# A hybrid decoder trunk on one core: the memory's row scales from loaded rows, and indexer scores of two heads' late rows in one matmul

## The chip, the core and the metric

The kernel runs on one core of one Trainium2 chip. A core has TensorE (PE in the profile, its weight loads PEld), VectorE (DVE), ScalarE (ACT), GpSimd (POOL) and SyncE (SP), which here only sends DMAs. Instructions of one engine run in the order in which they stand in its queue; engines wait for each other by semaphores. [...]

The metric is the device time of one execution in microseconds (us). Before the change three runs took 2596.93, 2597.0 and 2600.05 us; the median is 2597.0.

## The reference, cut to what matters

The trunk has four layers over 256 rows of 2048 features; mixers are latent attention, sparse attention, sliding window, latent attention. Each layer also attends with four heads to a memory of 256 rows. Two parts matter here.

First, the memory is normalised once, by rows, and every layer projects keys and values from it:

```python
mem_n = _rmsnorm(mem, mem_norm)      # y = x * rsqrt(mean(x*x, axis=-1) + EPS) * g
...
mem_out = _memory_attention(mq, mem_n @ w_mem_kv[i])
```

Second, the sparse mixer chooses 64 of 256 keys for each query row with an indexer of 16 heads of 64 numbers:

```python
k_top = min(IDX_TOPK_MAX, S // 4)    # 64
dots = jnp.einsum('bqhd,bkd->bqhk', iqb, ik, ...) * IDX_DIM ** -0.5
score = jnp.einsum('bqhk,bqh->bqk', jax.nn.relu(dots), iwb) * IDX_HEADS ** -0.5
score = jnp.where(qi[:, None] >= key_idx[None, :], score, NEG_INF)
_, sel = lax.top_k(score, k_top)
```

A query row below 64 has at most 64 keys that it may see, so all of them are chosen whatever the scores are. In the first tile of 128 query rows only the last 64 rows ("late rows") need scores.

## The kernel before

All matrices are float32. Each operand of a product is split into a high part, rounded to the type that TensorE reads at full rate, and a low part that holds the rest. A product is high x high + high x low + low x high. `parts_of` (L233) does this for weights: ScalarE copies 128x512 numbers to `wh` (L60), VectorE subtracts to get `wl` (L69), three buffers of each.

Weights stream from memory through five buffers `wr` of 512 KB (`stage`, L205); SP sends the loads. Two loops use them. `rows_by` (L239) gives rows of the result: features are stationary, a weight tile of 512 columns moves, three matmuls for each of 16 steps and two row tiles (L264 to L266). `columns_by` (L269) gives the result transposed: weights are stationary, both feature parts move together in 512 columns (L284), and the weights' low part takes 256 columns (L288). Each of the two holds two of the four accumulators (`acc`) in PSUM until its result is evicted.

The order of instructions on each engine comes from a planner, which runs through the program's order as priorities and issues what its own model of the times says is ready. `tc.keep_in_program_order` pins an instruction behind what was traced before it on its engine. Work that shall lie beside a matmul loop is written as a generator in the list `steps`; each loop calls `other_work` once per weight tile, which takes two steps (L228).

`memory()` (L363) comes first. The memory is given transposed as `l_mem`; four feature chunks `mft` (128x4x256, tag `pq`, five buffers) are loaded between the weights of the first `rows_by`, the values (`mv`) of layer 0's first half (`each`, L371; the last thing it sends is the constant `ident`), and are weighted and split in `prepare`. The row scale isn't needed for the product itself: it is applied when the accumulators are evicted, for values in `values` (L413) by rows with `mrstd`, for keys (`mk`) in `keys` (L423) by columns with `mbc`, which `spread` (L170) makes with two small products on TensorE. `row_scales` (L390) computes it from the feature chunks: four squares on ScalarE, pinned (L386), summed over chunks on VectorE (L388, L395, L396), summed over partitions on TensorE (`msr`, L400), then `rsqrt_mean` (L151), a chain of small VectorE instructions. It runs as steps in the first key block's `columns_by`; `values` of the first pass is one of its steps.

In layer 1, `select` (L802) computes the indexer's queries (`iqT`), keys (`ikd`) and head weights (`iw`). Twelve heads' queries of the first row tile are computed for its late rows alone (`stacked_late`); `iqT` holds zeros for the early rows of these heads, written by GpSimd (L809). High and low part of a head's 64 numbers lie on the two halves of the partitions, and `ikd` has the keys' high part twice and the low part twice in its two slices. `selection` (L856) is a generator of steps: for each row tile b and head, two matmuls of 256 columns (L865), Relu on ScalarE (L868), a scaled add on VectorE (L873). Then, eight times, the eight largest scores are found and taken out (L881, L882), and what remains becomes the mask `sel` (L885). At its end `spaced_values` makes the values' operand in the same buffers that `iqT` had. Its steps run in the loops of the memory queries, of the gate and of the first group's queries.

Of the kernel before, what the change touches and what calls it, by code (L numbers as in the profile page):

```python
# [31 lines left out]
def kernel(ctx: ExitStack, tc: tile.TileContext, a: dict, out: bass.AP,  # L32
# [39 lines left out]
    x = [cst.tile([P, D], F32, name=f"x{t}") for t in range(2)]  # L72
    xin = a["x"].rearrange("b (t p) d -> t p (b d)", p=P)


# [287 lines left out]
    def memory():  # L363
# [3 lines left out]
        mT = [act.tile([P, 2, 4, S], F32R, name="mT", tag=f"big{c}") for c in range(4)]  # L367
        sq = act.tile([P, 4, S], F32, name="msq", tag="aux", bufs=AUX)
        acc0 = []

# [11 lines left out]

        def squares(c):

            s1 = sq if c == 0 else act.tile([P, 4, S], F32, name="ms1", tag="aux", bufs=AUX)
            tc.keep_in_program_order(nc.scalar.activation(s1, mft[c].q, AF.Square))  # L386
            if c:
                nc.vector.tensor_add(sq, sq, s1)  # L388

        def row_scales():  # L390

            for c in range(4):
                squares(c)
                yield True
            nc.vector.tensor_add(sq[:, :2, :], sq[:, :2, :], sq[:, 2:, :])  # L395
            nc.vector.tensor_add(sq[:, 0, :], sq[:, 0, :], sq[:, 1, :])  # L396
            yield True
            pr = misc("msr")
            for t in range(2):
                nc.tensor.matmul(pr[:, t:t + 1], sq[:, 0, t * P:(t + 1) * P], ones[:, :1],  # L400
                                 start=True, stop=True)
            yield True
            s2 = small("ms2", 2)
            nc.vector.tensor_copy(s2, pr[:, :2])
            rsqrt_mean(mrstd, s2, D)
            nc.vector.tensor_scalar(m16, mrstd, 0.0625, None, op0=OP.mult)
            yield True
            values(0, 0, acc0[0])
            for _ in range(4):
                yield True  # L410
            spread(mbc, m16)
# [20 lines left out]
        for i in range(depth):  # L432
            w = a["w_mem_kv"][i]
            for p_ in range(2):
                begins = i == p_ == 0
                if begins:
                    pinned.append(0)
                    acc0.append(rows_by(mT, 16, w, 0, (MEMW, 512), "mv", prepare, each))
                    pinned.pop()
                    steps.append(row_scales())  # L440
                else:
                    values(i, p_, rows_by(mT, 16, w, 0, (MEMW + p_ * 512, 512), "mv"))
                for h in (2 * p_, 2 * p_ + 1):
                    acck = columns_by(mT, 16, w, 0, (h * 256, 256), "mk")
                    while begins and steps:
                        other_work()
                    keys(i, h, acck)
                step = 2 * i + p_
                if begins:

                    not_before(f32(mT[3])[:, 0, 3, :1])
                    late_constants()
                    bias_table(0)
                    bias_table(1)
                if 1 <= step < 5:
                    steps.append(nm.first_chunk(step - 1))


    def transposed(dst, srcs):

        for i0 in range(0, len(srcs), 4):
            i1 = min(len(srcs), i0 + 4)
            tp = misc("tr", F32R)
            for i in range(i0, i1):
                nc.tensor.transpose(tp[:, (i - i0) * P:(i - i0 + 1) * P], srcs[i], identr)
            copy_act(dst(i0, i1), f32(tp)[:, :(i1 - i0) * P].rearrange("p (j c) -> p j c", c=P))

# [275 lines left out]
    class Grouped:  # L743
# [46 lines left out]

        def stacked(self, dst, src, sc, n):

            s3 = src.rearrange("p (g d) -> p g d", g=n)
            for g0 in range(0, n, 4):
# [4 lines left out]
                transposed(lambda i0, i1: dst(g0 + i0, g0 + i1),  # L799
                           [hl[:, g].rearrange("p a b -> p (a b)") for g in range(4)])  # L800

        def select(self):  # L802
            nm, w = self.nm, self.w
            iqT = [act.tile([P, 8, S], F32R, name="iqT", tag=f"big{1 + z}") for z in range(2)]
            ikd = act.tile([P, 2, S], F32R, name="ikd", tag="kr", bufs=1)
            iw = small("iw", 32, bufs=2)

            for z, n in ((0, 8), (1, 4)):
                nc.gpsimd.memset(f32(iqT[z])[:, :n, :64], 0.0)  # L809
            late_x = act.tile([P, 16, 2, 64], F32R, name="xl64", tag="big3")  # L810
# [4 lines left out]
            for n in (8, 4, 4):  # L815
# [3 lines left out]
                for t in range(2):  # L819
                    sc = nm.col("rstd", t)  # L820
                    if late is not None and t == 0:
                        self.stacked_late(lambda i0, i1: iqT[h0 // 8][:, h0 % 8 + i0:h0 % 8 + i1, 64:P],
                                          acc[0][:, :n * 64], sc, n)
                        continue
                    sl = slice(t * P, (t + 1) * P)
                    self.stacked(lambda i0, i1: iqT[h0 // 8][:, h0 % 8 + i0:h0 % 8 + i1, sl],
                                 acc[t][:, :n * 64], sc, n)
                    if h0 == 12:
# [3 lines left out]
            nc.vector.tensor_scalar(iw, iw, 0.25, None, op0=OP.mult)  # L832
            return self.selection(iqT, ikd, iw)

# [20 lines left out]

        def selection(self, iqT, ikd, iw):  # L856

            for b in range(2):
                n = (b + 1) * P
                sco = [wk.tile([P, S], F32, name=f"sco{z}", tag=f"sco{z}", bufs=1) for z in range(2)]  # L860
                cur = 0
                for h in range(16):
                    sp = misc("isp")
                    for v in range(2):
                        nc.tensor.matmul(sp[:, :S], iqT[h // 8][:, h % 8, b * P:(b + 1) * P], ikd[:, v, :],  # L865
                                         start=v == 0, stop=v == 1)
                    rl = wk.tile([P, S], F32, name="rl", tag="e", bufs=4)
                    nc.scalar.activation(rl[:, :n], sp[:, :n], AF.Relu, scale=0.125)  # L868
                    c = iw[:, b * 16 + h:b * 16 + h + 1]
                    if h == 0:  # L870
# [5 lines left out]
                    yield True  # L876
                nc.vector.tensor_add(sco[1 - cur][:, :n], sco[cur][:, :n], caus[:, S - n:])
                cur = 1 - cur
                for it in range(8):
                    m8 = small("m8", 8)  # L880
                    nc.vector.max(m8, sco[cur][:, :n])  # L881
                    nc.vector.match_replace(sco[1 - cur][:, :n], m8, sco[cur][:, :n], TAKEN)  # L882
                    cur = 1 - cur
                    yield True
                nc.vector.tensor_scalar(self.sel[:, b, :n], sco[cur][:, :n], -2e38, NEG,  # L885
                                        op0=OP.is_gt, op1=OP.mult)
# [156 lines left out]
def _laid_out(inputs):  # L1043
# [6 lines left out]
    for name, o in (("mem_norm", 0), ("a_q_norm", 32), ("a_kv_norm", 56), ("norm_in", 64)):  # L1050
# [4 lines left out]

_INS = ["x", "final_norm", "rel_bias", "w_in_a", "w_uq",
        "w_ukv", "w_in_b", "w_in_c", "c_sinks", "w_mem_kv", "w_out"]
# [23 lines left out]
```

## Time and profile before

| | |
|---|---|
| runs | 2596.93, 2597.0, 2600.05 us |
| the profiled execution | 2597.13 us, of which the span 2595.3 |
| TensorE busy, share of the span | 2576.4 us, 99% |
| weight loads | 2216.7 us, 85% |
| VectorE | 1880.5 us, 72% |
| ScalarE | 1619.6 us, 62% |
| GpSimd | 68.0 us, 3% |
| mean granted TensorE clock | 0.998 |
| moved by DMA | 509.53 MB |

The busy time of TensorE is that of overlapping instructions: a matmul's own length is longer than the time by which it moves the next one. What a matmul costs is read from the chain that ended last, where each piece has only the time that it adds. A line number is that of the instruction in the code; where a helper records it (L60, L69, L202), the tile's name tells which use it is.

### The profile page before, as it was taken

Reading aid. Unit: us, or ns where it says so; the run is one execution under the profiler, and the core shown is the slowest. Engines: PE = TensorE matmul, PEld = TensorE weight load, DVE = VectorE, ACT = ScalarE, POOL = GpSimd, SP = SyncE. Lnnn points to the kernel's source line nnn. Section 1 sums busy time; section 2 is a strip of 40 time slices with the busy share of each in tenths; the row PEclk is TensorE's granted clock in tenths of the full one; section 3 lists DMA queues with packets and bytes.
Section 4 is the critical chain, followed back from the end, with each engine's and each line's share of the span. In section 5 each row is a group of like instructions: output and inputs, shape, how many; then the busy total and the mean of one; then the engine's idle time right before and its main releaser. Section 6 shows DMA issues by size and latency. Waiting matters only on the chain.

```text
span 2595.3 us, 41702 instructions
## 1 busy us (share of the span) xinstructions
PE 2576.4 (99%) x14066; PEld 2216.7 (85%) x14066; DVE 1880.5 (72%) x4130; ACT 1619.6 (62%) x3420; POOL 68.0 (3%) x124
## 2 busy tenths in 40 slices
PE   9999999999999999999999999999999999999997
PEld 7888898888888888888888888888888888888886
DVE  7666667667776686787778776777778767676667
ACT  6556556556656566667666666676666655665655
POOL 0100000000000010000000000000000000000000
PEclk9999999999999999999999999999999999999999
DMA  7888777666676667566556575555655766566664
GB/s 257 254 258 267 242 214 234 185 171 190 193 203 201 197 218 246 163 196 189 192 164 199 170 224 170 175 174 180 195 161 149 233 183 168 170 167 182 212 178 131
DMA packets 455128, 509.53 MB, mean 196 GB/s; under 512 B 68816, under 2 KB 351712, under 8 KB 453760
## 3 DMA queue, kind: packets, MB, share of 16 engines
q1 hardware_dynamic: 441392, 449.58, 57.9%
q0 software_dynamic: 13088, 56.16, 6.8%
q8 instruction: 110, 1.80, 0.3%
q10 hardware_dynamic: 432, 1.11, 0.1%
q14 instruction: 106, 0.87, 0.1%
HBM read 487.81 MB, written 31.56 MB: 200 GB/s over the span
## 4 chain that ended last, share of the span: by engine, by line
PE 99%; DVE 1%; ACT 0%; DMA 0%; SPq 0%; issue 0%; ACTq 0%
PE acc_g L284 14%; PE acc_g L288 7%; PE acc_wo L264 7%; PE acc_wo L265 7%; PE acc_wo L266 7%; PE acc_mk L284 5%; PE acc_mq L284 5%; PE acc_cq L284 3%; PE acc_qn L284 3%; PE acc_mq L288 2%; PE acc_mk L288 2%; PE acc_q L265 2%; PE acc_q L266 2%; PE acc_q L264 2%; PE acc_mv L265 2%; PE acc_mv L264 2%
## 5 line engine op out<-in xcount | busy, mean ns | idle before, releaser
L69 DVE TENSOR_TENSOR wl<-wr,wh 128x512 fp32r<-128x512 f32 (+2 forms) x1728 | 1165.0, 677 | 625.8 <-ACT wh L60 602.8
L60 ACT ACTIVATE wh<-wr 128x512 fp32r<-128x512 f32 (+2 forms) x1728 | 1070.4, 621 | 813.8 <-PE acc_g L284 179.3
L284 PE MATMUL acc_g<-xT,wh 128*128 128x512 f32 x1536 | 486.3, 396 | 0.0
L288 PEld LDWEIGHTS acc_g<-xT,wl 128*128 128x128 f32 x1536 | 284.8, 188 | 60.8
L288 PE MATMUL acc_g<-xT,wl 128*128 128x256 f32 x1536 | 310.5, 280 | 0.0
L265 PE MATMUL acc_wo<-wl,y 128*128 128x512 f32 x768 | 303.5, 395 | 0.2 <-DVE wl L69 0.2
L266 PE MATMUL acc_wo<-wh,y 128*128 128x512 f32 x768 | 298.2, 390 | 0.0
L284 PEld LDWEIGHTS acc_g<-xT,wh 128*128 128x128 f32 x1536 | 238.3, 189 | 4.4
L264 PE MATMUL acc_wo<-wh,y 128*128 128x512 f32 x768 | 240.1, 391 | 0.1
L265 PEld LDWEIGHTS acc_wo<-wl,y 128*128 128x128 f32 x768 | 144.3, 188 | 28.4 <-DVE wl L69 0.6
L266 PEld LDWEIGHTS acc_wo<-wh,y 128*128 128x128 f32 x768 | 144.3, 188 | 27.9
L264 PEld LDWEIGHTS acc_wo<-wh,y 128*128 128x128 f32 x768 | 142.2, 188 | 29.2 <-ACT y L60 1.0
L284 PE MATMUL acc_mk<-mT,wh 128*128 128x512 f32 x512 | 161.7, 396 | 0.3 <-DVE mv L418 0.3
L284 PE MATMUL acc_mq<-xT,wh 128*128 128x512 f32 x512 | 161.6, 396 | 0.0
L968 DVE TENSOR_TENSOR x<-x,acc_wo 128x512 f32<-128x512 f32 x192 | 126.1, 681 | 5.7 <-PE acc_wo L266 5.6
L284 PE MATMUL acc_qn<-cT,wh 128*128 128x512 f32 x384 | 121.2, 397 | 0.0
L284 PE MATMUL acc_cq<-xT,wh 128*128 128x512 f32 x384 | 120.8, 396 | 0.0
L288 PEld LDWEIGHTS acc_mk<-mT,wl 128*128 128x128 f32 x512 | 96.0, 188 | 22.3 <-DVE wl L69 0.4
L288 PEld LDWEIGHTS acc_mq<-xT,wl 128*128 128x128 f32 x512 | 94.0, 188 | 20.1
L288 PE MATMUL acc_mq<-xT,wl 128*128 128x256 f32 x512 | 103.3, 282 | 0.0
L288 PE MATMUL acc_mk<-mT,wl 128*128 128x256 f32 x512 | 101.9, 278 | 0.0
L265 PE MATMUL acc_q<-wl,xT 128*128 128x512 f32 x256 | 101.1, 395 | 0.0
(304 smaller groups left out, 4272.5 us busy)
## 6 DMA issues: line engine op xcount, KB each, us to landing
wr<-in_w_out_dram SPq DMA_DIRECT2D x192, 512.0 KB, 3.6
wr<-in_w_in_a_dram SPq DMA_DIRECT2D x176, 512.0 KB, 4.0
wr<-in_w_mem_kv_dram SPq DMA_DIRECT2D x120, 512.0 KB, 4.4
wr<-in_w_in_b_dram SPq DMA_DIRECT2D x112, 512.0 KB, 3.5
wr<-in_w_in_c_dram SPq DMA_DIRECT2D x104, 512.0 KB, 3.5
wr<-in_w_uq_dram SPq DMA_DIRECT2D x192, 128.0 KB, 2.5
wr<-in_w_uq_dram SPq DMA_DIRECT2D x48, 256.0 KB, 3.7
tab<-flat POOLq DMA_DIRECT2D x8, 1536.0 KB, 9.4
```

The costliest lines, as they stand in the source:

```text
L60: inst = nc.scalar.activation(o, i, AF.Copy, scale=scale)
L69: nc.vector.tensor_sub(lo, src, f32(hi))
L264: nc.tensor.matmul(acc[t][:, :n], xh, wh[:, :n], start=first, stop=False)
L265: nc.tensor.matmul(acc[t][:, :n], xh, wl[:, :n], start=False, stop=False)
L266: nc.tensor.matmul(acc[t][:, :n], xl, wh[:, :n], start=False, stop=last)
L284: nc.tensor.matmul(acc[j], wh[:, o:o + P], q[:, :, kt % 4, :], start=kt == 0, stop=False)
L288: nc.tensor.matmul(acc[j][:, 0, :], wl[:, o:o + P], q[:, 0, kt % 4, :], start=False, stop=kt == kts - 1)
L968: nc.vector.tensor_add(xs, xs, acc[t])
```

## The change

The memory's row scales. The memory is now an input in its own layout too (`mem`). Right after the first pass over the values has been traced, eight loads of 128x512 numbers (256 KB each) are pinned behind `ident` on SP's queue, into four tiles of the tag `pq`, which the feature chunks hold until they are split. After the whole first key block, in program order, `row_scales` squares each block on ScalarE with a sum along the row (`square_sum`, L202 of the kernel before), adds the four sums of each row on VectorE, and goes on as before to `rsqrt_mean` and `spread`; then `values` of the first pass are evicted, then the keys. The squares of the feature chunks, their sums on VectorE and the sum over partitions on TensorE are gone, and so are the steps.

Selection. `iqT` is now one tile for each row tile: for b = 0 16 heads x 64 late rows, for b = 1 16 heads x 128 rows. The last four heads of the first tile, which come for all rows, are transposed as before, and only the late half is copied out. For b = 0 the stationary operand holds the late rows of heads 2h and 2h + 1; the moving operand holds 128 keys' high parts and 128 keys' low parts, so one matmul of 256 columns gives both, side by side, where there were two matmuls for each head. ScalarE copies the one half, VectorE adds the other, then come Relu and the scaled add as before, for eight pairs instead of 16 heads. In the end the sum over even heads, on the first 64 partitions, is copied to the last 64 and added. Max, replace and mask work on the late rows alone; GpSimd clears the early rows of `sel`, and the clearing of `iqT` is gone.

```diff
+    min_ = a["mem"].rearrange("b (t p) d -> t p (b d)", p=P)
...
+        mss = small("mss", 8, bufs=2)
...
-        def squares(c):
-
-            s1 = sq if c == 0 else act.tile([P, 4, S], F32, name="ms1", tag="aux", bufs=AUX)
-            tc.keep_in_program_order(nc.scalar.activation(s1, mft[c].q, AF.Square))
-            if c:
-                nc.vector.tensor_add(sq, sq, s1)
-
-        def row_scales():
-
+        def memory_rows(c):
+            q = act.tile([P, 2, 512], F32, name="mrow", tag="pq", bufs=PQ)
+            for t in range(2):
+                tc.keep_in_program_order(
+                    nc.sync.dma_start(q[:, t, :], min_[t][:, c * 512:(c + 1) * 512]))
+            return q
+
+        def row_scales(mrow):
             for c in range(4):
-                squares(c)
-                yield True
-            nc.vector.tensor_add(sq[:, :2, :], sq[:, :2, :], sq[:, 2:, :])
-            nc.vector.tensor_add(sq[:, 0, :], sq[:, 0, :], sq[:, 1, :])
-            yield True
-            pr = misc("msr")
-            for t in range(2):
-                nc.tensor.matmul(pr[:, t:t + 1], sq[:, 0, t * P:(t + 1) * P], ones[:, :1],
-                                 start=True, stop=True)
-            yield True
+                for t in range(2):
+                    square_sum(mss[:, t * 4 + c:t * 4 + c + 1], mrow[c][:, t, :])
             s2 = small("ms2", 2)
-            nc.vector.tensor_copy(s2, pr[:, :2])
+            nc.vector.tensor_reduce(s2, mss.rearrange("p (t c) -> p t c", t=2), AX.X, OP.add)
             rsqrt_mean(mrstd, s2, D)
             nc.vector.tensor_scalar(m16, mrstd, 0.0625, None, op0=OP.mult)
-            yield True
-            values(0, 0, acc0[0])
-            for _ in range(4):
-                yield True
             spread(mbc, m16)
...
                     pinned.append(0)
-                    acc0.append(rows_by(mT, 16, w, 0, (MEMW, 512), "mv", prepare, each))
+                    acc = rows_by(mT, 16, w, 0, (MEMW, 512), "mv", prepare, each)
                     pinned.pop()
-                    steps.append(row_scales())
+                    mrow = [memory_rows(c) for c in range(4)]
...
                     acck = columns_by(mT, 16, w, 0, (h * 256, 256), "mk")
-                    while begins and steps:
-                        other_work()
+                    if begins and h == 0:
+                        row_scales(mrow)
+                        values(i, p_, acc)
                     keys(i, h, acck)
...
-            iqT = [act.tile([P, 8, S], F32R, name="iqT", tag=f"big{1 + z}") for z in range(2)]
+            iqT = [act.tile([P, 16, (64, P)[b]], F32R, name=f"iqT{b}", tag=f"big{2 - b}") for b in range(2)]
...
-            for z, n in ((0, 8), (1, 4)):
-                nc.gpsimd.memset(f32(iqT[z])[:, :n, :64], 0.0)
...
+            iw2 = small("iw2", 8, bufs=2)
+            pairs = iw[64:, :16].rearrange("p (h e) -> p h e", e=2)
+            for e in range(2):
+                nc.scalar.activation(iw2[64 * e:64 * e + 64], pairs[:, :, e], AF.Copy)
+            return self.selection(iqT, ikd, iw, iw2)
...
+            nc.gpsimd.memset(self.sel[:64, 0, :P], 0.0)
             for b in range(2):
                 n = (b + 1) * P
+                rows = slice(0, P) if b else slice(64, P)
...
-                for h in range(16):
+                for h in range((8, 16)[b]):
                     sp = misc("isp")
-                    for v in range(2):
-                        nc.tensor.matmul(sp[:, :S], iqT[h // 8][:, h % 8, b * P:(b + 1) * P], ikd[:, v, :],
-                                         start=v == 0, stop=v == 1)
                     rl = wk.tile([P, S], F32, name="rl", tag="e", bufs=4)
-                    nc.scalar.activation(rl[:, :n], sp[:, :n], AF.Relu, scale=0.125)
-                    c = iw[:, b * 16 + h:b * 16 + h + 1]
+                    if b == 0:
+
+                        nc.tensor.matmul(sp[:, :S], iqT[0][:, 2 * h:2 * h + 2, :].rearrange("p h c -> p (h c)"),
+                                         ikd[:, :, :P], start=True, stop=True)
+                        lo = wk.tile([P, S], F32, name="isl", tag="z", bufs=3)
+                        copy_act(lo[:, :P], sp[:, P:S])
+                        nc.vector.tensor_add(lo[:, :P], lo[:, :P], sp[:, :P])
+                        nc.scalar.activation(rl[:, :n], lo[:, :P], AF.Relu, scale=0.125)
+                        c = iw2[:, h:h + 1]
+                    else:
+                        for v in range(2):
+                            nc.tensor.matmul(sp[:, :S], iqT[1][:, h, :], ikd[:, v, :],
+                                             start=v == 0, stop=v == 1)
+                        nc.scalar.activation(rl[:, :n], sp[:, :n], AF.Relu, scale=0.125)
+                        c = iw[:, 16 + h:17 + h]
...
+                if b == 0:
+                    even = wk.tile([P, S], F32, name="isl", tag="z", bufs=3)
+                    nc.scalar.activation(even[64:, :n], sco[cur][:64, :n], AF.Copy)
+                    nc.vector.tensor_add(sco[cur][64:, :n], sco[cur][64:, :n], even[64:, :n])
```

29 lines of the change are left out of this document (13 added, 16 removed).

## The prediction

> **What bounds the kernel now.** I read the page's busy times first, then the chain that ended last, then stages of the span.
>
> ```profile
> span 2595.3 us, 41702 instructions
> PE 2576.4 (99%) x14066; PEld 2216.7 (85%) x14066; DVE 1880.5 (72%) x4130; ACT 1619.6 (62%) x3420; POOL 68.0 (3%) x124
> ```
>
> TensorE (PE) lacks 18.9 us of the span. Two windows hold nearly all that matters (columns: length, then busy time of PE, weight loads, VectorE, ScalarE, GpSimd, then granted clock, DMA share, GB/s):
>
> ```profile
> 41.00:45.00 4.00, 1.14 (x7) 0.84 (x7) 3.49 (x14) 2.31 (x5) 0.32 (x1) 1.00 0.46 135
> ...
> 45.00:500.00 455.00, 455.00 (x2459) 391.90 (x2458) 299.28 (x582) 264.57 (x510) 25.84 (x50) 1.00 0.77 239
> ...
> 2580.00:2596.00 16.00, 2.04 (x10) 1.35 (x8) 6.26 (x20) 3.57 (x6) 0.00 (x0) 0.67 0.33 132
> ```
>
> The last 14 us are the closing norm and the store, which the change leaves alone. In between PE does not rest, so two things count: matmul time that goes or comes, and stretches in which PE waits. One such stretch lies at 41 us, and the change rewrites exactly what stands there. The chain in order of time (start, length, what):
>
> ```profile
> 38.29 0.34 PE msr L400 x4
> ...
> 39.67 0.46 PE acc_mk L284 x2
> ...
> 40.37 0.48 PE acc_mk L284 x2
> 40.85 0.02 issue
> 40.87 0.64 ACT wh L60
> 41.53 0.69 DVE wl L69
> ...
> 42.92 0.17 DVE mrstd L166
> ...
> 43.11 0.70 ACT mv L60
> 43.83 0.76 DVE mv L418
> ...
> 44.64 0.50 PE acc_mk L284
> ```
>
> PE ends the first key block (mk of head 0) at 40.85 and can begin the next at 44.64. All four accumulators are taken: two by mk, two still by the values (mv), which wait for the memory's row scale. The chain is without PE for 44.64 - 40.85 = 3.79 us; what PE does inside it (the spread of the scale, L175) costs nothing.
>
> **The change: the memory's row scales.** *Removed.* Four squares of 128x1024 on ScalarE, five adds on VectorE, and PE's column sums (msr): 0.34 us of PE. The scale's small steps begin only after that sum, at 38.91 below, and end 4.2 us later (mrstd done at 43.09, two weight splits among them).
>
> ```profile
> 25.74 1.04 ACT L386 ACTIVATE msq<-ft 128x1024 f32<-128x1024 f32 x1
> ...
> 27.63 1.14 ACT L60 ACTIVATE wh<-wr 128x512 fp32r<-128x512 f32 x2
> ...
> 29.64 0.30 PEld L288 LDWEIGHTS acc_mk<-mT,wl 128*128 128x128 f32 x2 [0.37 <-DVE wl L69]
> ...
> 38.91 0.15 DVE L404 COPY ms<-msr 128x2 f32<-128x2 f32 x1
> ```
>
> *Added on SP's queue.* Eight loads of 256 KB stand behind ident and ahead of mk's first weights. SP's issues here:
>
> ```profile
> 11.70 0.93 SPq L213 DMA_DIRECT2D wr<-in_w_mem_kv_dram  x2
> 12.97 0.33 SPq L87 DMA_DIRECT2D ft<-in_l_mem_dram  x1
> 13.66 0.94 SPq L213 DMA_DIRECT2D wr<-in_w_mem_kv_dram  x2
> 14.95 0.33 SPq L87 DMA_DIRECT2D ft<-in_l_mem_dram  x1
> 15.67 0.96 SPq L213 DMA_DIRECT2D wr<-in_w_mem_kv_dram  x2
> 16.97 0.33 SPq L376 DMA_DIRECT2D ident<-in_c_ident_dram  x1
> 17.70 55.19 SPq L216 DMA_DIRECT2D wr<-in_w_mem_kv_dram  x20
> ```
> ```profile
> wr<-in_w_mem_kv_dram SPq DMA_DIRECT2D x1, 256.0 KB, 5.3
> ...
> wr<-in_w_mem_kv_dram SPq DMA_DIRECT2D x1, 512.0 KB, 5.8
> ```
> ```profile
> 12.00:16.00 4.00, 4.00 (x20) 3.29 (x19) 3.83 (x8) 3.38 (x8) 0.00 (x0) 1.00 1.02 372
> 16.00:20.00 4.00, 4.00 (x19) 3.31 (x18) 3.18 (x7) 3.02 (x7) 0.00 (x0) 1.00 1.05 382
> ...
> 20.00:28.86 8.86, 8.86 (x41) 7.32 (x40) 6.44 (x12) 7.55 (x14) 0.00 (x0) 1.00 0.93 293
> ```
> ```profile
> L60 ACT ACTIVATE mT<-ft,gvec x16: 493/494/511, 4.6 to 24.4; 128x256 fp32r<-128x256 f32 x16
> ```
>
> The second load of the 11.70 pair (issued at 12.3) took 5.3 us and so landed at 17.6; the issue at 17.70 is the eighth after it. The DMA engines are full (share 1.02 to 1.05), and in this stretch SP sends a load when the eighth before it has landed: three loads of 256 KB per 2.0 us, 0.67 us each. Now mk's first weights are issued at 17.70 and land 5.8 us later, at 23.5. With the eight row loads ahead they land 8 x 0.67 = 5.4 us later, at 28.9. They are split on ScalarE at 27.63 today; the second part's matmul (L288) starts at 29.64. After: 28.9 + 0.64 (wh) + 0.69 (wl) is 30.2 to 30.4, so PE waits about 0.7 us. This is the price of the transfers; until then 4.1 us of lead (23.5 to 27.6) cover them. Bounds: nothing, if the planner lets the unpinned weight loads pass the last row block, whose buffer comes free late (it needs the third feature chunk read, and the 16 reads, four to a chunk, run from 4.6 to 24.4, so near 20); and 2.5 us, if they land as far apart as at the 293 GB/s that the stretch from 20 us shows (2.1 MB in 7.2 us). I take 0.7, by the full stretch, which is where they run. Later weight tiles are asked for at once and catch up: a tile lasts PE 2.8 us (four steps of 0.70, 39.67 to 40.37 above) and transfers in two times 0.67.
>
> [...]
>
> *Added on ScalarE.* Eight squares of 128x512 with a row sum. The nearest rows are the same helper's (L202) on x:
>
> ```profile
> L202 ACT ACTIVATE junk<-x x40: 612/618/633, 109.4 to 2583.0; 128x512 f32<-128x512 f32 x40
> ...
> 109.38 0.63 ACT L202 ACTIVATE junk<-x 128x512 f32<-128x512 f32 x1 [1.05 <-DMA x<-in_x_dram]
> ...
> 979.98 0.44 PE spr L175 x4
> ```
>
> One per 0.71 us with its read of the sum (109.38 to 110.09), 5.7 us in all, against 4.2 before. Hidden: PE wants a split of 0.64 us every second step, 1.40 us, so ScalarE has 0.76 us free in each, and about 3 us at a stretch between its last split of the values' pass (near 25.7) and mk's weights (28.9). The row blocks land at about 22.6 to 27.3. So four squares fit before 29 and four go into later gaps, to about 34.
>
> *Moved.* Reduce and scale now stand in program order behind all of mk head 0, without the sum over PE. From 34 the same 4.2 us give the scale at 38 to 39, then 0.70 + 0.76 for the first value block: 40 to 40.5, while PE needs it at 40.85 + 0.7 - 0.34 = 41.2. So the stall of 3.79 us goes, by a margin of a microsecond; late next is nothing, or this same chain (a rival below). Waiting behind it on ScalarE are value copies and splits; who waits is PE's next accumulator. The spread, hidden in the stall until now, then lies on PE's path: 0.44 us (979.98 above), nothing if a rest of the stall remains. VectorE loses five adds of up to 128x1024, off the path. POOL issues the value stores some 3 us earlier, with nobody waiting for them.
>
> **The change: selection.**
>
> ```profile
> 1050.74 0.95 PE isp L865 x8
> ...
> L865 PE MATMUL isp<-ikd,iqT x64: 274/283/287, 1050.6 to 1117.3; 128*128 128x256 f32 x64
> L868 ACT ACTIVATE rl<-isp x32: 258/322/395, 1051.1 to 1117.8; 128x128 f32<-128x128 f32 x16, 128x256 f32<-128x256 f32 x16
> L873 DVE SCALAR_TENSOR_TENSOR sco<-rl,iw,sco x30: 344/414/486, 1052.2 to 1118.8; 128x128 f32<-128x128 f32 x15, 128x256 f32<-128x256 f32 x15
> ...
> 1065.00:1079.00 14.00, 14.00 (x85) 12.31 (x84) 13.11 (x42) 6.98 (x14) 0.00 (x0) 1.00 0.57 178
> ```
>
> The first row tile had 16 heads x 2 matmuls of 256 columns; it will have 8 of the same width. On the chain one costs 0.95/8 = 0.119 us, so 24 x 0.119 = 2.85 us of PE go, and nothing covered them. (283 ns is one matmul's pipelined length, not its cost.) Transposes stay in number: the late rows are cut out at eviction. ScalarE trades 16 Relus (258 ns) for 8 copies and 8 Relus of the same shape; VectorE trades 16 scaled adds (344) for 8 and 8 plain adds of that width; five small edge steps (two weight columns, the even half, its add, the cleared mask) are estimated at the Relu's 0.26 us each. All beside PE. Two memsets of GpSimd go, one comes; its queue waits anyway. A PSUM tile is now held through copy and add, some 0.5 us longer; heads come four at a time about 4 us apart, which covers it. Eight of 48 planner steps vanish, so selection ends earlier; the values' spacing waits for it and comes earlier too.
>
> **Sum**, against the profiled execution (2597.13 us: span 2595.3 and 1.83 around it): -3.79 - 0.34 + 0.44 + 0.7 - 2.85 = -5.84, thus **2591.3 us**. The median of the runs shown is 2597.0, the same within 0.01%.
>
> **Rivals.**
> *The stall stays in part.* The planner gives the scale's steps whatever VectorE leaves; they, values and keys now meet in one stretch, and one 0.7 us split more ahead of each of them eats the margin. For it: the two splits inside today's chain. Against: the squares' rows are there by 27.3, and five adds of VectorE are gone. Price 0.5 to 3.8 us, thus 2592 to 2595.
> *ScalarE is stuck behind a square, and the kernel gets slower.* The row squares aren't pinned, as the old ones were. Where the planner believes rows landed sooner than they do, a square stands ahead of the split that PE needs. The 109.38 row is that mechanism: 1.05 us idle on ScalarE for x. The first rows land at 22.6. A square put at time t into the values' pass holds ScalarE to 23.3, and PE's lead there is an estimated 2 us (the pass's last split is over by the square at 25.74; its six matmuls at 0.24 us each must begin near 27.6 to be done when mk begins near 29), so PE loses 21.3 - t. It decides from a loss of 5.8 us, t below 15.5; squares put near t = 13 would give 2599.8. Against: 1.05 us is the longest such wait on rows in this trace, and PE felt none of it.
> [...] Today's 3.79 us wait shows granted clock 1.00 in its window and in the next.
> *Selection fills VectorE.* Eight steps fewer bring the max/replace rounds and the second tile's heads closer together; at 1065 to 1079 VectorE is busy 13.11 of 14 us already. If a weight split is late there, 1 to 3 us come back: 2592.3 to 2594.3. Against: in that very window PE stands full at 14.00.
>
> **Chances.** Forecast 0.57 (its own range 2589.5 to 2592.5: no lateness of weights and the spread still hidden, or half a microsecond more of each); stall in part 0.24; stuck ScalarE 0.12; VectorE 0.07. A measurement of this kernel tells about 0.2%, 5.2 us, from no change; the forecast lies just beyond that. Faster by more than it: most of the forecast's share, 0.48. Slower by more: the stuck case with the stall kept as well, 0.09. Else 0.43. The range reaches from 2589.0 to 2596.5 and leaves out the worst of the stuck case.
>
> **What would show it.** PE without a gap between 40 and 46; no msr; isp 40 times instead of 64, still near 0.12 each on the chain; eight squares between 24 and 35; mk's first weights landing near 29, with a PE wait below a microsecond before the first L288 of mk. Wrong, if ScalarE idles on the row loads before 25, if mrstd comes after 41, or if PE shows new waits at 1050 to 1140.

## The result, and the profile after

| | before | after |
|---|---|---|
| median, range | 2598.74 (2596.93 to 2600.05), 17 runs | 2593.01 (2591.56 to 2594.19), 17 runs |
| ratio, 95% interval | | 0.9978 (0.9970 to 0.9985) |
| the profiled execution | 2597.13 | 2594.19 |

The medians differ by 5.7 us, against 5.84 forecast; the time itself was forecast as 2591.3 and came out 1.7 us higher. The two profiled executions differ by 2.9 us only. That of before was one of the shortest of its kernel, that of after the longest of its 17. Where these offsets come from is the larger part of what follows.

The head of the page after, and its windows (length; busy time of PE, weight loads, VectorE, ScalarE, GpSimd; granted clock, DMA share, GB/s):

```profile
span 2592.4 us, 41637 instructions
...
PE 2574.6 (99%) x14038; PEld 2213.6 (85%) x14038; DVE 1875.6 (72%) x4126; ACT 1619.6 (62%) x3435; POOL 67.3 (3%) x123
```
```profile
41.00:45.00 4.00, 4.00 (x26) 3.56 (x25) 3.42 (x9) 2.51 (x6) 0.72 (x2) 1.00 0.87 252
45.00:500.00 455.00, 453.68 (x2447) 389.69 (x2446) 297.00 (x579) 263.32 (x509) 24.95 (x48) 1.00 0.77 238
```

The stall at 41 us is gone: PE is busy 4.00 of 4.00 us, where it had 1.14. But in the next row PE now rests for 1.32 us, and before it rested for none. PE's own instructions, in order of time, show the place of the old stall:

```profile
40.54 0.63 PE L285 MATMUL acc_mk<-mT,wh 128*128 128x512 f32 x2
41.01 0.40 PE L289 MATMUL acc_mk<-mT,wl 128*128 128x256 f32 x2
41.24 0.61 PE L176 MATMUL spr<-dg,ones 128*128 128x128 f32 x4
41.60 0.48 PE L285 MATMUL acc_mk<-mT,wh 128*128 128x512 f32 x1
```

The spread of the scale (`spr`) now stands on PE's path, between two key blocks, with no wait around it. How the scale got there in time is read from SP's queue, ScalarE, PE and VectorE, each in order of time:

```profile
17.49 0.33 SPq L376 DMA_DIRECT2D ident<-in_c_ident_dram  x1
18.17 3.72 SPq L387 DMA_DIRECT2D mrow<-in_mem_dram  x6
22.26 0.93 SPq L217 DMA_DIRECT2D wr<-in_w_mem_kv_dram  x2
23.28 1.25 SPq L387 DMA_DIRECT2D mrow<-in_mem_dram  x2
24.62 3.34 SPq L217 DMA_DIRECT2D wr<-in_w_mem_kv_dram  x3
```
```profile
23.93 0.62 ACT L203 ACTIVATE junk<-mrow 128x512 f32<-128x512 f32 x1
...
28.44 0.62 ACT L203 ACTIVATE junk<-mrow 128x512 f32<-128x512 f32 x1
...
29.05 1.66 ACT L60 ACTIVATE wh<-wr 128x512 fp32r<-128x512 f32 x3
...
31.99 0.61 ACT L203 ACTIVATE junk<-mrow 128x512 f32<-128x512 f32 x1
...
38.96 1.25 ACT L60 ACTIVATE mv<-acc_mv,mrstd 128x512 fp32r<-128x512 f32 x2
```
```profile
29.37 0.39 PE L267 MATMUL acc_mv<-wh,mT 128*128 128x512 f32 x1
29.72 0.74 PE L285 MATMUL acc_mk<-mT,wh 128*128 128x512 f32 x2
30.45 0.50 PE L289 MATMUL acc_mk<-mT,wl 128*128 128x256 f32 x2
```
```profile
32.73 0.16 DVE L395 TENSOR_REDUCE ms<-mss 128x2 f32<-128x8 f32 x1
...
38.30 0.15 DVE L167 SCALAR_TENSOR_TENSOR mrstd<-rw,ry 128x2 f32<-128x2 f32 x1
...
39.70 1.40 DVE L405 SCALAR_TENSOR_TENSOR mv<-acc_mv,mrstd,mv 128x512 fp32r<-128x512 f32 x2
```

Two loads of weights (512 KB each, issued at 22.26) passed the last row block on SP's queue. The squares run from 23.9 to 32.6, none waits for its rows, and six of the eight are done when the key block's weights come at 29.05. The scale stands at 38.45, both value blocks are out at 41.10, and PE takes up the next key block at 41.60.

In the selection, the tile's view has 8 + 32 matmuls where it had 64, and the chain of waits still shows 0.12 us for each:

```profile
L872 PE MATMUL isp<-ikd,iqT x32: 274/278/283, 1054.0 to 1084.6; 128*128 128x256 f32 x32
...
L863 PE MATMUL isp<-ikd,iqT x8: 277/283/333, 1044.9 to 1053.8; 128*128 128x256 f32 x8
```
```profile
1049.33 0.36 PE isp L863 x3
...
1054.12 0.48 PE isp L872 x4
```

These 0.12 us are for 256 columns of the rounded type. The two products of the spread, of unrounded f32 and 128 columns each, add 0.44 us to the chain, recorded as four (at 979.98 in the prediction's rows).

What has grown are waits of ScalarE in the loops after the first. The row of ScalarE's waits on `x`, before and after, then its instructions in time and PE's:

```profile
ACT junk L202 <- DMA x<-in_x_dram: 1.6, 2, 1.1
```
```profile
ACT junk L203 <- DMA x<-in_x_dram: 5.7, 5, 2.5
```
```profile
196.76 0.63 ACT L203 ACTIVATE junk<-x 128x512 f32<-128x512 f32 x1 [2.51 <-DMA x<-in_x_dram]
...
198.04 1.13 ACT L60 ACTIVATE wh<-wr 128x512 fp32r<-128x512 f32 x2
```
```profile
198.71 0.73 PE L265 MATMUL acc_mv<-wh,mT 128*128 128x512 f32 x2 [1.10 <-ACT wh L60]
```

A square of x rows, which the change doesn't touch, stands ahead of a weight split that PE needs, and waits 2.51 us for its rows; PE then waits 1.10 us. The kernel before has the same squares; its profile shows 1.6 us of such waits, in two places, and none of PE behind them.

To see what belongs to what, I cut every profiled execution of this study at five points: the start of the last matmul of the first values' pass (`acc_mv`, near 29), the start of the second values' pass (near 55), the first `acc_kva` (near 367, where the memory phase is over), the last `acc_iq` (near 1033), and the last `acc_kv` near 1523. Lengths in us between these points, each the difference of two start times in the views of these tiles; the kernels are told in the next section:

| kernel | startup | head of the memory phase | its other loops | to the indexer | selection and on | rest |
|---|---|---|---|---|---|---|
| before | 28.9 | 27.1 | 311.1 | 666.8 | 490.8 | 1070.7 |
| before_b | 29.3 | 28.0 | 313.3 | 666.7 | 490.8 | 1070.7 |
| e_warm | 28.6 | 27.0 | 314.5 | 666.7 | 490.8 | 1070.6 |
| b_pin | 29.5 | 28.5 | 310.8 | 666.8 | 490.8 | 1070.7 |
| b_pinwarm | 28.7 | 27.1 | 310.8 | 666.7 | 490.8 | 1070.7 |
| e_sel | 29.9 | 28.1 | 311.9 | 666.7 | 488.0 | 1071.0 |
| after | 29.4 | 23.5 | 313.4 | 667.2 | 488.4 | 1070.6 |
| again | 28.4 | 23.5 | 311.9 | 667.2 | 488.3 | 1070.6 |
| e_mem | 29.3 | 23.5 | 313.0 | 667.2 | 491.2 | 1070.6 |
| e_pin | 29.6 | 23.9 | 310.8 | 667.2 | 488.3 | 1070.6 |
| e_late | 29.7 | 28.1 | 313.3 | 667.2 | 488.3 | 1070.6 |
| e_twice | 29.7 | 26.2 | 312.5 | 667.2 | 488.4 | 1070.6 |

From before to after: startup +0.5, head -3.6, other loops +2.3, to the indexer +0.4, selection -2.4, rest -0.1, together -2.9. The head and the selection move the way that the prediction said. The startup and the loops aren't part of its sum, and they vary between executions of one and the same kernel. The way to the indexer isn't in the sum either, but it does not vary: 666.7 to 666.8 in the six profiles with the old row scales, 667.2 in the six with the new.

### The profile page after: what moved, and what is told of

Read it like the earlier page. It is cut to its first block, busy times and chain, and to the rows that moved or that the text cites. A ratio compares the mean times of both kernels' runs of the same rounds, so it can differ in the third digit from the quotient of the medians.

```text
span 2592.4 us, 41637 instructions
## 1 busy us (share of the span) xinstructions
PE 2574.6 (99%) x14038; PEld 2213.6 (85%) x14038; DVE 1875.6 (72%) x4126; ACT 1619.6 (62%) x3435; POOL 67.3 (3%) x123
## 4 chain that ended last, share of the span: by engine, by line
PE 91%; DVE 0%; ACT 0%; issue 0%; ACTq 0%
PE acc_g L285 14%; PE acc_g L289 7%; PE acc_wo L265 7%; PE acc_wo L266 7%; PE acc_wo L267 7%; PE acc_mq L285 5%; PE acc_cq L285 3%; PE acc_qn L285 3%; PE acc_mq L289 2%; PE acc_mk L285 2%; PE acc_q L266 2%; PE acc_q L267 2%; PE acc_q L265 2%; PE acc_cq L289 2%; PE acc_qn L289 2%; PE ptp L487 1%
## 5 line engine op out<-in xcount | busy, mean ns | idle before, releaser
L266 PEld LDWEIGHTS acc_wo<-wl,y 128*128 128x128 f32 x768 | 144.3, 188 | 28.4 <-DVE wl L69 0.6
```

The costliest lines, as they stand in the source:

```text
L266: nc.tensor.matmul(acc[t][:, :n], xh, wl[:, :n], start=False, stop=False)
```

## The experiments

My theory: the change gives what the sum says, and the profile after is short of it because x rows come late for squares that the planner has put too early (theory A). The rivals: the earlier squares of the memory or the larger traffic cause those waits and so take back part of the gain for good; and, added after the first runs, that the kernel before loses more at 41 us than its one profile shows (theory C).

### The changed kernel again

No edit.

> The changed kernel once more, for a second profile. In its first profile ScalarE idled 4.1 us in the third and fourth value passes (150 to 200 us) behind squares of x rows that hadn't landed, and PE lost some 2.2 us there between the landmarks at 188 and 234 us. Theory A (that wait is a matter of the single run, set by how fast x lands): the waits on x differ clearly from 5.7 us in all, and the span differs by about as much as PE loses there. Theory B (it is fixed by the order of instructions): 5 to 6 us of waits again, and the same place of the loss. The time beside the kernel before: about 5.7 us less under both.

Measured 2593.0 (2591.68 to 2594.36), ratio 0.9977 (0.9968 to 0.9986). The profiled execution took 2591.77, waits on x rows are 3.7 us in place of 5.7, and PE's list has no wait behind them. What follows: the waits differ from execution to execution, by an amount (loops 311.9 against 313.4) that explains most of the 2.4 us between the two profiles of this kernel; the rest is the startup.

### Each part alone

`e_mem` has the memory's part of the diff, with the old selection; `e_sel` the selection's, with the old memory.

```diff
-                for h in range(16):
+                for h in range((8, 16)[b]):      # e_sel; e_mem keeps range(16)
...
-                    steps.append(row_scales())
+                    mrow = [memory_rows(c) for c in range(4)]      # e_mem; e_sel keeps the steps
```

> Only the memory's row scales are changed; selection is as before. By the sum (-3.79 -0.34 +0.44 +0.7) 3.0 us less than the kernel before; by the first profile's landmarks 3.7 less at the start of the second value pass, of which up to 2.2 come back where ScalarE waits for x rows, so 1.5 to 3.7 less. Rival: the stall at 41 us was not worth its length, because what it let run ahead is now missed, and the gain of the whole change is selection's: no change within 0.5 us. isp stays at 64.

> Only selection is changed; the memory's row scales are as before. By the sum 24 matmuls of 0.119 us go: 2.85 us less than the kernel before; PE's stall at 41 us stays at 3.8 us on the chain, msr stays. Rival (VectorE fills up and weight splits come late): 0 to 1.5 us less, with new PE waits between 1040 and 1140 us.

Measured: memory part 2595.68 (ratio 0.9989, 0.9980 to 0.9998), selection 2597.55 (0.9993, 0.9984 to 1.0002), beside 2599.35 for the kernel before in the same runs: -3.7 and -1.8, together -5.5 where both give -6.35. The interval of the selection alone does not tell it from no change. The parts add up within what these medians can tell. By the table each does its own: 27.1 to 23.5 in the head for the one, 490.8 to 488.0 in the selection for the other.

The profile of `e_sel` showed something else. It has the old wait at 41 us, and its chain of waits goes on from there so:

```profile
44.68 1.22 PE spr L175 x4
45.90 0.55 PE acc_mk L284
46.45 0.21 PE acc_mk L288
46.66 0.43 PE acc_mk L284
```

The last of these matmuls adds 0.43 us alone, where the prediction's rows had 0.48 for two of its kind. The windows of the profile say why: granted clock 0.91 at 43 to 45, 0.50 at 45 to 47, 0.73 at 47 to 49 (shown below for two other runs). In the profile of before it was 1.00.

### The squares of x rows pinned

```diff
-        nc.scalar.activation(junk[:, :src.shape[-1]], src, AF.Square, accum_out=col)
+        inst = nc.scalar.activation(junk[:, :src.shape[-1]], src, AF.Square, accum_out=col)
+        if pinned:
+            tc.keep_in_program_order(inst)
...
             for t in range(2):
+                pinned.append(c)
                 square_sum(self.ss[:, t * 4 + c:t * 4 + c + 1], x[t][:, c * 512:(c + 1) * 512])
+                pinned.pop()
```

> The changed kernel with the squares of x rows pinned behind what was traced before them on ScalarE, so that the planner can't put them ahead of the weight splits. Theory A/B alike: no ScalarE wait on x rows, no PE wait in 100 to 260 us, so up to 2.2 us less than the changed kernel: about 2591 where that is 2593. Rival: the wait costs PE nothing beyond its buffers' lead in most runs: no difference to the changed kernel within 0.5 us.

Measured 2591.55 (2590.98 to 2592.15, seven executions), ratio 0.9971 (0.9960 to 0.9982); the changed kernel beside it 2593.0. ScalarE has no wait on x rows any more. Windows of `e_pin` and of after over the same 50 us:

```profile
150.00:200.00 50.00, 50.00 (x252) 42.41 (x251) 32.14 (x55) 28.92 (x54) 2.12 (x4) 1.00 0.84 272
```
```profile
150.00:200.00 50.00, 48.68 (x241) 40.06 (x240) 29.98 (x54) 29.32 (x57) 2.12 (x4) 1.00 0.80 258
```

PE is full, and the loops take 310.8 us. Theory A holds for the loops: the loss comes from the place of these squares on ScalarE; the loads are the same in both. Nor do the earlier squares of the memory or its larger traffic show in these waits: they come to 1.6, 5.0, 6.0 and 4.1 us in the four profiles with the old row scales and free squares (before, `before_b`, `e_warm`, `e_sel`), and to 3.7 to 5.7 us in the five with the new. This version is the fastest of the study, 1.5 us below the changed kernel (the two intervals overlap) and with a range of 1.2 us in place of 2.7.

### The kernel before again, and kept warm

`before_b` is the kernel before. `e_warm` gives PE something to do in its wait:

```diff
+            wd = misc("wd")
+            for _ in range(10):
+                tc.keep_in_program_order(nc.tensor.matmul(wd[:, :P], ones, ones, start=True, stop=True))
             spread(mbc, m16)
```

> The kernel before once more, for a second profile. The profile with only selection changed, whose row scales are those of before, showed the granted clock at 0.91, 0.50 and 0.73 in three windows of 2 us after PE's wait at 41 us, and PE's first eight matmul pairs after it at twice their time; the first profile of before showed 1.00 there. [...] Rival (that one profile was disturbed): 1.00 and a span near 2595 to 2597 whose excess lies elsewhere.

> The kernel before with ten small matmuls of constants, pinned on PE behind the first key block and ahead of the spread, that is, into PE's wait at 41 us. They compute nothing that is used and take about 2.2 us of the 2.8 us that PE idles there. Theory C (executions lose up to 2 us by the clock after that wait): granted clock 1.00 at 43 to 49 us in the profile, and the median 1 to 2 us under that of before. Rival (the wait alone costs, no clock): the median of before within 0.5 us, or up to 0.5 us more where the added matmuls outlast the wait.

Measured: 2600.15 (ratio 1.0004, 0.9995 to 1.0013) and 2599.27 (0.9999, 0.9990 to 1.0008), that is, no difference in the medians. The windows of `before_b`, the same two stretches of the first profile of before, and those of `e_warm`:

```profile
43.00:45.00 2.00, 0.96 (x4) 0.93 (x4) 1.80 (x7) 1.50 (x3) 0.00 (x0) 0.66 0.65 235
45.00:47.00 2.00, 2.00 (x8) 1.69 (x7) 1.66 (x4) 0.42 (x2) 0.97 (x2) 0.50 0.40 146
```
```profile
43.00:45.00 2.00, 1.08 (x6) 0.84 (x7) 1.90 (x7) 1.81 (x4) 0.32 (x1) 1.00 0.45 173
45.00:47.00 2.00, 2.00 (x13) 1.77 (x12) 1.93 (x5) 0.42 (x1) 0.89 (x2) 1.00 0.60 223
```
```profile
43.00:45.00 2.00, 1.37 (x8) 1.07 (x8) 1.93 (x6) 1.70 (x4) 0.54 (x1) 1.00 0.32 123
45.00:47.00 2.00, 2.00 (x14) 1.74 (x13) 1.93 (x6) 0.42 (x1) 0.67 (x2) 1.00 0.71 254
```

One kernel, two executions: behind the same wait the clock stays in one and is halved in the other, and at 45 to 47 PE gets through 8 matmuls in place of 13. With the filler the clock stays, and the head takes 27.0 us as in the first profile. But the loops then took 314.5 us, with waits on x rows of 6.0 us. The median that I had forecast, 1 to 2 us less, did not come. So the run couldn't price the clock: what it had gained in the head was less than what the x rows vary by. That called for the pin in both kernels (below).

### The row loads later

```diff
-                    mrow = [memory_rows(c) for c in range(4)]
                 ...
                     acck = columns_by(mT, 16, w, 0, (h * 256, 256), "mk")
                     if begins and h == 0:
+                        mrow = [memory_rows(c) for c in range(4)]
                         row_scales(mrow)
```

> The changed kernel with the eight row loads traced behind the first key block's weights instead of ahead of them. Theory (transfers ahead of mk's weights cost their lateness, and the scale has a margin of only about 1 us): mk begins without a wait, 0.3 to 0.7 us earlier against the end of the values' pass; the rows land 4 to 6 us later, the scale near 41 to 42, so PE waits 1 to 2.5 us ahead of the second key block; in sum 0.5 to 2 us more than the changed kernel, near 2594.5. Rival (the place of the loads doesn't matter, the margin is wider): within 0.5 us of the changed kernel, no PE wait at 41.

Measured 2598.52 (2595.52 to 2600.64), ratio 0.9997 (0.9988 to 1.0006): 5.5 us above the changed kernel, much more than I had expected. All of the head's gain is gone, 28.1 us. From the list of PE's waits, and ScalarE in time:

```profile
PE spr L176 <- DVE dg L175: 2.6, 1, 2.6
```
```profile
32.98 0.63 ACT L203 ACTIVATE junk<-mrow 128x512 f32<-128x512 f32 x1 [1.08 <-DMA mrow<-in_mem_dram]
...
38.82 0.62 ACT L203 ACTIVATE junk<-mrow 128x512 f32<-128x512 f32 x1
...
44.11 1.26 ACT L60 ACTIVATE mv<-acc_mv,mrstd 128x512 fp32r<-128x512 f32 x2 [1.64 <-DVE mrstd L167]
```

The loads were issued at 25.1 to 30.6 in place of 18.2 to 24.1, the last square runs at 38.82 in place of 31.99, and the values are evicted 5.2 us later. That is the old stall again, with the old wait of 2.6 us before the spread, and behind it the clock fell (0.50 at 45 to 47). I had put the scale at 41 to 42; it stands at 44.07. The last row block landed 6.3 us later (37.55 in place of 31.28), where I had 4 to 6, and the margin that takes up a later landing is about half a microsecond (in the changed kernel the values are out at 41.10, PE goes on at 41.60).

### Twice the row loads

```diff
                     mrow = [memory_rows(c) for c in range(4)]
+                    for c in range(4):
+                        extra = act.tile([P, 2, 512], F32, name="mextra", tag="aux", bufs=AUX)
+                        for t in range(2):
+                            tc.keep_in_program_order(
+                                nc.sync.dma_start(extra[:, t, :], min_[t][:, c * 512:(c + 1) * 512]))
```

> The changed kernel with eight more loads of the same 256 KB behind the row loads, into tiles that nothing reads. Theory (a full DMA stretch passes on 0.67 us per load, and PE waits for what the weights' lead doesn't cover): 5.4 us more of transfers ahead of mk's third or first weight tile, PE waits 2.5 to 5 us more in the first key block, the kernel 2 to 5 us slower than the changed one, near 2596. Rival (weights pass the extra loads or there is bandwidth left): under 1 us.

Measured 2597.04 (2594.81 to 2599.66), ratio 0.9992 (0.9983 to 1.0001), 4.0 us above the changed kernel. PE's wait, the window in which it lies, and the chain of waits there:

```profile
PE acc_mk L285 <- ACT wh L60: 1.9, 1, 1.9
```
```profile
36.00:41.00 5.00, 3.04 (x16) 2.10 (x15) 4.04 (x8) 3.12 (x6) 1.21 (x2) 1.00 1.09 354
```
```profile
31.94 6.14 DMA wr<-in_w_mem_kv_dram
```

The head takes 26.2 us, 2.7 more; where the rest of the 4.0 lies, this one profile does not show. The 4.0 us are inside what I had put down (2 to 5); PE's wait of 1.9 us is below it (2.5 to 5). The queue's slack at this place is thus less than one more set of 2.1 MB: the eight loads of the change cost nearly nothing, the next eight cost a wait for weights. In this run the wait lies at 36 to 41, two weight tiles further on than the first one that could be late: its load goes out at 31.94, behind the extra ones.

### The pin on the kernel before, without and with the filler

Both edits are shown above: `b_pin` is the kernel before with the squares of x rows pinned, `b_pinwarm` has the ten products as well.

> The kernel before, with one edit of another place: the squares of x rows keep their place in program order on ScalarE, as the weighted parts beside them do. Theory A (the waits of ScalarE on x rows cost PE 1 to 2 us in either kernel): 1 to 2 us faster than the kernel before, 2597.5 to 2598.5; no ScalarE wait on x rows in the profile; the wait at 41 us stays, with or without a lower clock behind it. Theory B (the pin helps only together with the earlier scale): no change, within 0.5 us.

> The kernel before, with the x rows' squares pinned and ten products of constants ahead of the spread in the wait at 41 us, so that PE isn't idle there for long. Theory C (the clock falls behind that wait in most executions, and the warm run gave the gain back in waits on x rows): 1 to 2 us faster than the kernel with the pin alone, 2596 to 2597, granted clock 1.00 at 41 to 52 us, values' pass of the second head at 55.6 to 56.2. Rival (the clock's price is hidden by the rest of the chain there): no change against the kernel with the pin alone, within 0.5 us.

Measured 2598.52 (2596.78 to 2598.84), ratio 0.9995 (0.9986 to 1.0004), and 2596.82 (2596.41 to 2597.92), ratio 0.9991 (0.9982 to 1.0000). Windows of the two profiles:

```profile
45.00:47.00 2.00, 1.73 (x6) 1.50 (x6) 1.97 (x6) 0.59 (x3) 1.12 (x2) 0.50 0.26 98
```
```profile
45.00:47.00 2.00, 2.00 (x14) 1.72 (x13) 1.93 (x6) 0.42 (x1) 0.77 (x2) 1.00 0.68 242
```

With the pin the loops take 310.8 us in both, as in `e_pin`, whatever stands in the head. Then the clock can be seen in the times: the eleven executions of `b_pin` fall into two groups, four from 2596.78 to 2597.22 and seven from 2598.36 to 2598.84. The profiled one is in the upper group, and its clock was halved. With the filler all eleven lie below 2598. The median falls by 1.7 us, and the head is 1.4 us shorter in the profile, as long as in the first profile of before, whose clock had stayed. Theory C holds. That the two groups of `b_pin` are those with and without the fall is inferred from their times; one profiled execution, in the upper group, shows it. Their distance (1.6 us between the means, 2597.0 and 2598.6) need not be the clock alone: the startup, which has no part in this, varies from 28.4 to 29.9 us over the twelve profiles, and the eleven times with the filler spread over 1.5 us.

The views of all seven profiles that have the old wait, or the filler in it, side by side (PE's wait before `spr` from its list of waits, the rest from their windows):

| profile | wait before `spr`, us | PE busy at 41 to 45, us | clock at 43 to 45 | at 45 to 47 | at 47 to 49 |
|---|---|---|---|---|---|
| before | 2.6 | 1.14 | 1.00 | 1.00 | 1.00 |
| before_b | 2.6 | 1.41 | 0.66 | 0.50 | 0.99 |
| e_sel | 2.6 | 1.40 | 0.91 | 0.50 | 0.73 |
| e_late | 2.6 | 1.37 | 0.82 | 0.50 | 0.83 |
| b_pin | 2.6 | 1.40 | 1.00 | 0.50 | 0.65 |
| e_warm | 0.4 | 3.37 | 1.00 | 1.00 | 1.00 |
| b_pinwarm | 0.4 | 3.37 | 1.00 | 1.00 | 1.00 |

In the first five the wait has the same length, and PE was busy least at 41 to 45 in the one whose clock stayed. So neither number tells that execution from the four others, and what does is not shown. `e_twice`, where PE waits for weights for 1.9 us at 36 to 41, shows 1.00 in every window from 36 to 49.

The pin itself gave the kernel before 0.6 us by the medians (2599.09 to 2598.52) and 1.2 by the means, less than the 1 to 2 us that I had put down; the interval doesn't tell it from nothing.

## Why the prediction was right, point by point

**The stall of 3.79 us goes, the spread comes in its place.** Right, and shown by PE's rows at 40 to 42. With the column sums gone and the spread in, the head was to shrink by 3.79 + 0.34 - 0.44 - 0.7 = 2.99 us. It shrank by 3.6 between the two profiles, from 27.1 to 23.5.

**The weights behind the row loads come 0.7 us late.** Over-sized. PE's two rows from 29.37 to 30.45 hold the key block up by about 0.3 us (its first pair adds 0.73 us where 0.46 is usual). The prediction had named the reason as a bound: the planner let two loads of weights pass the last row block. By the trace, even the 0.3 us are not the landing's: the first of these loads landed at 28.48 (issued at 22.26, 6.2 us on the way), and ScalarE began to split it at 29.05, when the sixth square was done. The speed was not the reason. The stretch 17 to 30 us, in the view of the DMA:

```profile
DMA packets 3125, 4.60 MB, mean 354 GB/s; under 512 B 258, under 2 KB 1454, under 8 KB 3123
```

This is below the 372 and 382 that I had used; at 354 the 2.1 MB take an estimated 5.9 us, and the wait in program order would have been 1.2 us. The order of the loads saved the sum. `e_twice` shows what loads cost there when they aren't hidden: 2.7 us in the head. The rate differs from stretch to stretch: 8 to 12 us of the same trace show 397 GB/s.

**The squares fit, and the scale comes at 38 to 39.** Right: 38.45, from the first square at 23.93 on. Six were done ahead of the weights, not four. The margin of one microsecond was half of that, and `e_late` shows how little that is: later loads brought the whole stall back.

**24 matmuls of 0.119 us, 2.85 us.** Right. The stretch shrank by 2.8 us with the selection alone (before to `e_sel`) and by 2.9 where the memory's part was in already (`e_mem` to after). That it is only 2.4 from before to after is the memory's part: `e_mem` is 0.4 us longer there than before (491.2 against 490.8), and the kernels with the new row scales also take 0.4 us more on the way to the indexer. PE has no wait on that way and one of 0.2 us in the selection's stretch, in before as in after. Laid over each other, the matmuls of before and `e_mem` drift apart evenly: `e_mem` is ahead by 1.3 us at 450 us, by 0.9 at 1000 and by 0.5 at 1500, with no step at any one place. The sum has no term for this, and its cause stays open.

**The rivals.** *The stall stays in part*: no. *VectorE fills up*: no, no wait of PE there. *ScalarE is stuck behind a square*: the mechanism is real, its place was wrong. (By its own terms a square near 13 would have given 2591.3 + 8.3 = 2599.6, not 2599.8.) The memory's squares, for which I had worked it out, never waited in the changed kernel. The squares of x rows in the loops behind did, and cost PE 1.32 us in the profiled execution (0.22 and 1.10). I had used their row (1.05 us at 109.38) as a model, and hadn't asked whether it could itself grow. The sum lacks this term. But it isn't a price of the change alone: `before_b` has 5.0 us of these waits and loops of 313.3. The pin took 1.5 us off the changed kernel and 0.6 off the kernel before, so that up to 0.9 us may be the change's own; the intervals don't settle it.

**The clock.** I gave the clock no term, since the wait at 41 us showed 1.00 in its window and the next. That was one execution. In four other profiles with that wait (`before_b`, `e_sel`, `e_late`, `b_pin`) the clock was at 0.50 at 45 to 47; in the three of them that have the old row scales the head took 28.0 to 28.5 us in place of 27.1. Removing the wait removes that price too: `after`, `again`, `e_mem` and `e_pin` show 1.00 in every window from 36 to 49. The step of mine that failed is that one profile stood for the kernel. The 3.79 us of which I spoke there are the chain's; PE was idle for only 2.6 us of them, before the spread. What tells the execution at 1.00 from the four at 0.50, no run shows.

**The time.** By the table, head -3.6, way to the indexer +0.4 and selection -2.4 make -5.6, against -5.84 in the sum. That this is so near is in part luck: the head gave 0.6 us more than its terms, and the even drift behind it took 0.8 us that had no term. The sum was laid on 2597.13, an execution in which the clock had stayed and the loops ran at 311.1, so the forecast is the time of an undisturbed execution. `e_pin`, whose loops are free of waits on x rows, took 2591.55, 0.25 us from it. The changed kernel's median is 1.7 us above the forecast, and the pin gives 1.5 us of that back; the median lies 0.5 us beyond the own range of the likeliest case, inside the full range. The median of before is 1.6 us above 2597.13, and pin and filler together bring it to 2596.82. The two offsets have different causes, x rows in the one, mostly the clock in the other. That they nearly cancel, so that the difference of the medians, 5.7, is almost that of the sum, is luck. Between the pinned kernels the medians differ by 5.3 us where the filler keeps the clock up (`b_pinwarm` to `e_pin`), and by 7.0 where it doesn't (`b_pin` to `e_pin`). Faster by 0.22%, the change stands just beyond the 0.2% that I called measurable, as forecast.

## What to carry to other kernels

A wait that is gone may be worth more than its length: here the granted clock behind it was 0.50 in four profiles of five. Look at the clock behind a wait in more than one execution, since one profile can fall on the good side, as the first one did here (1.00). Work without a pinned place that depends on a load is a risk on an in-order engine, however small: the planner puts it where the rows ought to be there, and whoever is queued behind pays when they aren't (here 2.51 us of ScalarE, and 1.10 us of PE behind it). When stretches of the program are cut at fixed points, as in the table, the parts that the change moves stand out from those that vary by themselves.

## What the runs showed that I had not expected

- PE was idle for 2.6 us in the wait at 41 us (the wait before `spr`), and the clock granted at 45 to 47 was 1.00 in one execution and 0.50 in four others. The price was 0.9 to 1.4 us in the head. With ten products of constants in the wait, PE waited 0.4 us before `spr`, and the clock was 1.00, both times that they were tried.
- The same loads of x rows made ScalarE wait between 1.6 and 6.0 us in all, in nine profiles of kernels with these squares left free (1.6 and 5.0 in two executions of the kernel before, 5.7 and 3.7 in two of the changed kernel). Pinned, they never did, in the profiles of three kernels.
- The margin of the change is narrow on both sides of the same queue: loads 6.5 to 7 us later cost 5.5 us, 2.1 MB more cost 4.0.
